# Where the weight parts of the Strassen-like products begin in their tiles: 208 bytes in place of 64

## The chip, the cores and the metric

The kernel runs on one core of one Trainium2 chip. The metric is the device time of one execution in microseconds (us), as the median of several runs. The page names five engines: PE (TensorE, matrix products), PEld (the same engine's weight loads, which overlap its products), DVE (VectorE), ACT (ScalarE) and POOL (GpSimd). SP issues most transfers.

## The reference, cut to what matters

The model is a decoder trunk with two layers over 512 tokens of width 1024. The first layer mixes tokens with a gated delta rule, the second with sliding-window attention, and both also attend to 256 memory tokens. Each layer ends in a feed-forward block, which is where the change acts:

```
def swiglu(h, w_gate_up, w_down):
    gu = h @ w_gate_up
    return (jax.nn.silu(gu[..., :D_FF]) * gu[..., D_FF:]) @ w_down
...
x = x + swiglu(rms_norm(x, ln_ffn[layer]), w_gate_up[layer], w_down[layer])
```

`h` is 512 tokens by 1024, `w_gate_up` is 1024 by 5632 and `w_down` 2816 by 1024, all in float32.

## The kernel before, in words

**A product in three parts.** The kernel multiplies in a rounded float32 type (float32r). To keep the precision, each operand is split into a high part (the rounded value, written by ACT, line 148) and a low part (what the rounding left, written by DVE, line 161), and a product is the sum of three: high by high, high weight by low activation, low weight by high activation. This is `mm3`, whose products are all line 154. In each of them a block of 128 by 128 weights is the stationary operand, loaded by PEld, and the activations stream past it.

**Wide and narrow products.** Most projections stream 512 tokens at a time, so a wide product is 128x512. In the feed-forward blocks most of the gate and up columns go through another path, `quarters`: a column of weights is cut in two halves of features and the tokens in two halves, and sums and differences of the quarters take the place of some of the products, as in Strassen's method. Those products are narrow, 128x256, and their weight parts are made by `product` inside `quarters`. Each call of `product` splits one half column of weights (128x512) and then runs four `mm3`, twelve narrow products of PE. Its activations are either halves of the tiles `h` and `l`, or the tiles `T`, which hold split sums of tokens made once by `token_sums`. The results go to the PSUM banks `g`.

**The ring.** `weight` and `quarters` share tiles of two tags, `whi` and `wlo`, with three buffers each. A tile holds 1024 numbers and `SPARE` = 64 more, 4352 bytes of each partition. `weight` uses a tile from its first byte. `quarters` takes its places from `ring`: three pairs of tiles, with two places each, the first at number `SHIFT` of the tile, the second 512 numbers behind it. A place is used again after six calls.

**Where the operands lie.** In the built program the three `whi` tiles are at bytes 20416, 24768 and 29120 of each partition and the three `wlo` tiles at 33472, 37824 and 42176. Each of these leaves 192 when divided by 256, since a tile's 4352 bytes are 17 times 256. The activations `h`, `l`, `T`, and the memory tokens `mh` and `ml`, begin at addresses that leave 192 as well, and the pieces read of them lie whole multiples of 512 bytes further. So every wide product, and every narrow one over memory tokens at the kernel's start, reads weights and activations that both leave 192. In this kernel the ring's weights leave 0 (192 + 64 = 256).

**What sets the order.** Each engine works through its own instructions in the order in which the program was written; semaphores hold an instruction back until its inputs are there and its buffer is free. In `quarters` SP and POOL issue the transfers of the weight quarters (POOL's add to what is there), ACT writes the high part, DVE the low part, and PE's twelve products follow. ACT also copies some results out of PSUM (`held`, line 148, tile `fs`), and DVE joins the rest. `quarters` is called forty times, each time for two columns, and makes seven products for them: 280 calls of `product`, 3360 narrow products. Eight gate columns take the wide path instead. In each layer the ring runs in two stretches, and each is followed by the wide down projection; the seventh product of a pair comes after the next pair's first steps, so that the last one of a stretch lies inside the down projection.

Of the kernel before, what the change touches and what calls it, by code (L numbers as in the profile page):

```python
# [27 lines left out]
FT = DFF // P  # L28
EPS = 1e-6
LINE = 64  # L30
SHIFT, SPARE = 16, 64
NEG = -1e30
BASE = 32
NB = P // BASE
# [1236 lines left out]
```

## Time and profile before

| what | value |
|---|---|
| median of 3 runs | 1158.72 us (1157.88 to 1160.98) |
| the profiled execution, its own time | 1156.72 us |
| its span | 1155.0 us |
| granted TensorE clock | 0.998 |

The span runs from the first to the last instruction; the profiled execution's own time is 1.72 us longer. The page lists busy times and shares by engine, the same in 40 slices, the chain of work that ended last, and the costliest groups. A busy time of PE is the union of products that overlap: a narrow product is shown as 0.28 us long, but one starts about every 0.12 us. What counts for PE is therefore the distance between two starts, called pitch below.

### The profile page before, as it was taken

The numbers are of one execution on the slowest core, as the hardware profiler recorded it, in microseconds if no ns is written. First come the engines' busy times: TensorE is split into PE (matmuls) and PEld (weight loads), VectorE is DVE, ScalarE is ACT, GpSimd is POOL, SyncE is SP. The second block draws the span as 40 slices with busy tenths as digits, with TensorE's granted clock in tenths as the row PEclk, the third lists the DMA queues.
The fourth block names the chain that finished last, engine by engine and source line by source line (L and its number), as shares of the span: only waits on it lengthen the run. The fifth ranks groups of instructions, "written<-read, shape, count | busy, mean of one in ns | idle before, by whom it ended". The sixth has DMA issues, their size and how long they took to land.

```text
span 1155.0 us, 19665 instructions
## 1 busy us (share of the span) xinstructions
PE 1131.5 (98%) x7476; PEld 992.9 (86%) x7476; DVE 842.6 (73%) x1587; ACT 631.7 (55%) x1271; POOL 86.0 (7%) x97
## 2 busy tenths in 40 slices
PE   7999999999999999999999999999999999999996
PEld 6888778887899998899998777777899988999986
DVE  6754877767789987389866767859799843898754
ACT  7579563366556652256654547675566522566533
POOL 0310000000101100011100000010011100111000
PEclk9999999999999999999999999999999999999999
DMA  8434342225657744567723421144477733577232
GB/s 309 133 106 117 113 103 98 92 92 165 168 139 190 188 123 126 154 147 188 178 70 104 137 73 38 51 107 126 110 188 191 183 109 105 141 183 188 72 94 94
DMA packets 73971, 152.83 MB, mean 132 GB/s; under 512 B 17756, under 2 KB 18420, under 8 KB 73876
## 3 DMA queue, kind: packets, MB, share of 16 engines
q1 hardware_dynamic: 62356, 130.59, 36.2%
q0 software_dynamic: 11520, 20.98, 11.7%
q8 instruction: 59, 0.97, 0.4%
q14 instruction: 36, 0.29, 0.1%
HBM read 144.58 MB, written 6.96 MB: 131 GB/s over the span
## 4 chain that ended last, share of the span: by engine, by line
PE 85%; DVE 8%; ACT 3%; DMA 3%; issue 1%; SPq 0%; DVEq 0%; ACTq 0%
PE pj L154 40%; PE g L154 38%; PE sc L154 5%; DVE wlo L161 2%; ACT sm L142 1%; PE pt L158 1%; DMA wraw<-in_wout 1%; PE qk L154 1%; ACT whi L148 1%; PE g L158 1%; DVE l L164 1%; DMA wraw<-in_wmk 1%; DVE btmp L161 1%; DVE stats L778 1%; DVE big L161 1%
## 5 line engine op out<-in xcount | busy, mean ns | idle before, releaser
L148 ACT ACTIVATE whi<-wraw 128x512 fp32r<-128x512 f32 (+2 forms) x331 | 244.1, 745 | 256.1 <-PE pj L154 155.9
L161 DVE TENSOR_TENSOR wlo<-wraw,whi 128x512 fp32r<-128x512 f32 (+2 forms) x331 | 274.6, 839 | 104.6 <-ACT whi L148 98.6
L154 PE MATMUL pj<-h,whi 128*128 128x512 f32 (+1 forms) x676 | 266.5, 396 | 0.0
L154 PE MATMUL pj<-l,whi 128*128 128x512 f32 (+1 forms) x676 | 264.9, 392 | 0.5 <-DVE l L164 0.4
L154 PE MATMUL pj<-h,wlo 128*128 128x512 f32 (+1 forms) x676 | 264.3, 391 | 0.0
L154 PE MATMUL g<-T,whi 128*128 128x256 f32 x1280 | 230.2, 281 | 0.0
L154 PEld LDWEIGHTS g<-T,whi 128*128 128x128 f32 x1280 | 197.5, 190 | 1.7 <-DVE fu L164 1.7
L154 PE MATMUL g<-T,wlo 128*128 128x256 f32 x640 | 179.9, 281 | 0.0
L154 PEld LDWEIGHTS pj<-h,whi 128*128 128x128 f32 x676 | 126.8, 188 | 29.2 <-issue 3.6
L154 PEld LDWEIGHTS pj<-l,whi 128*128 128x128 f32 x676 | 127.2, 188 | 27.8 <-issue 1.8
L154 PEld LDWEIGHTS pj<-h,wlo 128*128 128x128 f32 x676 | 127.1, 188 | 25.6 <-issue 0.8
L154 PE MATMUL g<-l,whi 128*128 128x256 f32 (+1 forms) x508 | 146.1, 288 | 0.0
L154 PE MATMUL g<-h,whi 128*128 128x256 f32 (+1 forms) x508 | 146.0, 287 | 0.0
L154 PE MATMUL g<-h,wlo 128*128 128x256 f32 (+1 forms) x508 | 145.9, 287 | 0.0
L154 PEld LDWEIGHTS g<-T,wlo 128*128 128x128 f32 x640 | 120.2, 188 | 0.0
L154 PEld LDWEIGHTS g<-l,whi 128*128 128x128 f32 x508 | 97.4, 192 | 1.4 <-issue 0.2
L154 PEld LDWEIGHTS g<-h,whi 128*128 128x128 f32 x508 | 95.4, 188 | 1.2
L154 PEld LDWEIGHTS g<-h,wlo 128*128 128x128 f32 x508 | 95.4, 188 | 1.0
L1014 POOL DMA_DIRECT2D ws<-in_wgu x40 | 35.4, 884 | 700.9 <-ACT sq L151 244.5
L148 ACT ACTIVATE whi<-ws 128x512 fp32r<-128x512 f32 x80 | 50.5, 631 | 51.3 <-PE g L154 42.1
L161 DVE TENSOR_TENSOR fu<-pj,rstd 128x512 f32<-128x512 f32 (+1 forms) x34 | 22.4, 660 | 54.3 <-PE pj L154 54.3
L161 DVE TENSOR_TENSOR wlo<-ws,whi 128x512 fp32r<-128x512 f32 x80 | 54.9, 686 | 6.9 <-ACT whi L148 6.8
(345 smaller groups left out, 1617.2 us busy)
## 6 DMA issues: line engine op xcount, KB each, us to landing
wraw<-in_wgu SPq DMA_DIRECT2D x48, 512.0 KB, 4.3
ws<-in_wgu SPq DMA_DIRECT2D x80, 256.0 KB, 3.7
ws<-in_wgu POOLq DMA_DIRECT2D x80, 256.0 KB, 4.8
wraw<-in_wdn SPq DMA_DIRECT2D x48, 384.0 KB, 3.1
wraw<-in_win SPq DMA_DIRECT2D x26, 512.0 KB, 3.6
wraw<-in_wgu SPq DMA_DIRECT2D x40, 256.0 KB, 4.2
wraw<-in_wout SPq DMA_DIRECT2D x16, 512.0 KB, 3.7
wraw<-in_wdn SPq DMA_DIRECT2D x16, 256.0 KB, 2.7
```

What stands on the lines that cost most here:

```text
L142: ins = self.nc.scalar.activation(out, in_, func, **kw).ins
L148: self.copied = self.nc.scalar.activation(out, in_, AF.Copy, **kw).ins
L154: return self.nc.tensor.matmul(out, lhsT, rhs, start=start, stop=stop, skip_group_check=more).ins
L158: return self.nc.tensor.transpose(out, in_, self.ident[:k, :k]).ins
L161: return eng.tensor_tensor(out=out, in0=a, in1=b, op=op).ins
L164: self.nc.vector.scalar_tensor_tensor(out=out, in0=in0, scalar=scalar, in1=in1, op0=op0, op1=op1)
L778: nc.vector.tensor_reduce(out=mx[:, i:i + 2], in_=ps[b], op=ALU.max, axis=AX.X)
L1014: nc.gpsimd.dma_start(s1, a22, accum_op=ALU.add)
```

## The change: what it does, and the diff

`SHIFT` goes from 16 to 52 numbers. The ring's places then begin at bytes 208 and 2256 of their tiles in place of 64 and 2112. The tiles keep their size (the second place ends at number 1076 of 1088), so no tile moves, and no other operand does. The ring's weights then leave 400 - 256 = 144 when divided by 256, and their activations, at 192, lie 48 bytes further on modulo 256; before it was 192. The 280 high parts that ACT writes, the 280 low parts of DVE and the 3360 narrow products that read them get other addresses. The instructions of all engines, their order and their semaphores stay as they are.

```
-SHIFT, SPARE = 16, 64
+SHIFT, SPARE = 52, 64
```

The one place that uses it (line 898, in `ring`):

```
places.extend(tuple(x[:, SHIFT + i * T:SHIFT + (i + 1) * T] for x in two) for i in range(2))
```

## The prediction

> **What bounds the kernel now.** I read the engines first, then the chain, then PE's groups by form.
>
> ```profile
> span 1155.0 us, 19665 instructions
> PE   7999999999999999999999999999999999999996
> PEclk9999999999999999999999999999999999999999
> PE 85%; DVE 8%; ACT 3%; DMA 3%; issue 1%; SPq 0%; DVEq 0%; ACTq 0%
> PE pj L154 40%; PE g L154 38%; PE sc L154 5%; DVE wlo L161 2%; ACT sm L142 1%; PE pt L158 1%; DMA wraw<-in_wout 1%; PE qk L154 1%; ACT whi L148 1%; PE g L158 1%; DVE l L164 1%; DMA wraw<-in_wmk 1%; DVE btmp L161 1%; DVE stats L778 1%; DVE big L161 1%
> ```
>
> PE is busy in nearly every slice at the full granted clock, and 85% of the chain is PE. Its two great parts are the wide products (pj, 40%) and the products into g (38%), which are nearly all the ring's. The groups by form count them:
>
> ```profile
> L154 PE MATMUL g<-T,whi 128*128 128x256 f32 x1280 | 230.2, 281 | 0.0
> L154 PE MATMUL g<-T,wlo 128*128 128x256 f32 x640 | 179.9, 281 | 0.0
> L154 PE MATMUL g<-h,wlo 128*128 128x256 f32 x480 | 135.0, 281 | 0.0
> L154 PE MATMUL g<-l,whi 128*128 128x256 f32 x480 | 134.9, 281 | 0.0
> L154 PE MATMUL g<-h,whi 128*128 128x256 f32 x480 | 134.9, 281 | 0.0
> ```
>
> These are 1280 + 640 + 3 x 480 = 3360 products, the ones whose weights move. All have no idle time of PE ahead of them. The windows show the four stretches in which the ring runs, and a short one inside the first:
>
> ```profile
> core 0: us, PE busy (x) PEld busy (x) DVE busy (x) ACT busy (x) POOL busy (x), PEclk, DMA share, GB/s
> 340.00:430.00 90.00, 90.00 (x767) 90.00 (x766) 80.51 (x146) 56.15 (x107) 12.96 (x15) 1.00 0.67 166
> 500.00:590.00 90.00, 90.00 (x766) 90.00 (x766) 80.18 (x144) 56.63 (x109) 12.94 (x15) 1.00 0.68 164
> 830.00:920.00 90.00, 90.00 (x767) 90.00 (x766) 80.39 (x144) 56.23 (x108) 16.32 (x19) 1.00 0.76 185
> 990.00:1080.00 90.00, 90.00 (x766) 90.00 (x765) 80.81 (x146) 56.80 (x110) 12.94 (x15) 1.00 0.67 165
> 345.00:365.00 20.00, 20.00 (x172) 20.00 (x172) 18.67 (x34) 12.55 (x24) 3.45 (x4) 1.00 0.80 193
> ```
>
> PE never stops there. Of the 767 products in the first row two began before the window, so the pitch (start to start) is 90.00 / 765 = **117.65 ns**. The other rows give the same. The ring's share of the time is 3360 x 117.65 ns = 395 us, and every nanosecond of pitch is worth 3.36 us. Whatever the change does to the time, it does by this pitch, or by making DVE (80.51 of 90 us) the bound.
>
> **Does the pitch depend on addresses at all?** The trace holds four other cases of the same kind of product. Times are starts in us.
>
> ```profile
> 28.21 0.28 PE L154 MATMUL sc<-mh,whi 128*128 128x256 f32 x1
> ...
> 33.49 0.28 PE L154 MATMUL sc<-mh,wlo 128*128 128x256 f32 x1
> ...
> 321.69 0.39 PE L154 MATMUL pj<-h,whi 128*128 128x512 f32 x1
> ...
> 332.57 0.28 PE L154 MATMUL g<-h,whi 128*128 128x256 f32 x1
> ...
> 430.09 0.40 PE L154 MATMUL pj<-h,whi 128*128 128x512 f32 x1
> ...
> 431.02 0.40 PE L154 MATMUL pj<-l,whi 128*128 128x512 f32 x1
> ...
> 924.15 0.39 PE L154 MATMUL g<-T,whi 128*128 128x256 f32 x2
> ...
> 925.17 0.40 PE L154 MATMUL pj<-h,wlo 128*128 128x512 f32 x1
> ```
>
> - Narrow products over memory tokens, weights and activations both at 192 modulo 256, so 0 apart: 44 steps between 28.21 and 33.49, 5.28 / 44 = **120.0 ns**.
> - Wide products, 0 apart as well: 48 steps from 321.69 to 332.57, 10.88 / 48 = 226.7 ns. They stream 256 columns more than those for 226.7 - 120.0 = 106.7 ns, which is 0.417 ns a column. So 256 columns alone are 106.7 ns, and both kinds lose 13.3 ns more per product, however long they are. The ring at 192 apart loses only 117.65 - 106.7 = 11.0.
> - Nine of the ring's own products after a stop of PE, at the very same addresses as the others: from 924.15 to 925.17 (a row x2 is two products), 1.02 / 9 = **113.3 ns**, a loss of 6.6. The same is seen after the stop at 431 us.
> - Wide products just ahead of such a stop: 0.93 / 4 = 232.5 ns from 430.09 to 431.02, 5.8 more than in their steady state.
>
> I read this so: while one product streams, the weights of the next are loaded, and the two readings get in each other's way by an amount that depends on how they meet. It is set by the distance of the addresses (13.3 against 11.0) and by the phase in which PE has fallen in (11.0 against 6.6, same addresses). Both can hold for a hundred us.
>
> The Trainium skill speaks against this. Its page "TensorE: Matmul & The Clock Gate", section "Step-by-step: what each phase is for", gives PE two independent read ports and says that loading the next weights takes no read bandwidth from the running product. By that rule the change is worth nothing, 1158.7 us. The rows disagree as far as they go: one form has 120.0, 117.65 and 113.3 ns.
>
> **The change part by part.** Nothing is added, removed or reordered on any queue, so there is no new wait. Three kinds of access move.
>
> *The 280 high parts of ACT and the 280 low parts of DVE* are written 144 bytes further. What a start off the 64-byte grid costs is bounded by these rows:
>
> ```profile
> L164 DVE SCALAR_TENSOR_TENSOR l<-x,gains,h 128x512 fp32r<-128x512 f32 x32 | 23.5, 747 | 1.5 <-ACT h L148 1.5
> L164 DVE SCALAR_TENSOR_TENSOR qv<-pj,gains,qv 128x511 f32<-128x511 f32 x12 | 9.0, 746 | 2.7 <-ACT qv L148 2.4
> L148 ACT ACTIVATE whi<-ws 128x512 fp32r<-128x512 f32 x80 | 50.5, 631 | 51.3 <-PE g L154 42.1 <-ACT fs L148 9.2
> L148 ACT ACTIVATE h<-fu 128x512 fp32r<-128x512 f32 x32 | 20.2, 633 | 18.6 <-DVE fu L161 9.8 <-DVE fu L164 8.8
> ```
>
> The convolution's DVE step starts 4 bytes off the grid (511 columns) and takes 746 ns against 747 on it. ACT takes 631 ns to the ring's address and 633 to `h`, at 192. I take nothing. The cover is PE: a ring product of twelve lasts 12 x 117.65 = 1412 ns, 63.7 of them fill 90 us, and DVE works 80.51 / 63.7 = 1264 ns in each, ACT 881. Even 100 ns more on either would be hidden.
>
> *The 3360 narrow products.* No row has weights and activations 48 bytes apart, or weights that start off a multiple of 64. Bounds: no loss at all, 106.7 ns, would be 36.8 us faster; 120.0 with the extra 5.8 of the disturbed wide products, 125.8 ns, 27.4 us slower. The middle rows are 113.3, 117.65 and 120.0. By nearness alone 48 is closest to distance 0 and its 120.0 ns. I nevertheless take **113.3**, as the likeliest single value: these very products have run at it, so a loss of 11.0 isn't needed by them, and the one distance measured apart from 0 loses less than 0 does, so that I expect of another one that it too keeps the two readings out of each other's way, more or less well. This is a choice between rows, not a derivation, and the chances below say so.
>
> The sum: about 30 products are at 113.3 already, so 3330 x (117.65 - 113.3) = 14.5 us less. At 113.3 a ring product lasts 1360 ns. DVE's 1264 still fits; in the busiest window (345 to 365 us) it is 18.67 / 20 x 1412 = 1318, so 97% full there, and I give back 0.5 us for waits of PE on a low part. 1156.7 - 14.0 = 1142.7 for a profiled execution. The median lies 2.0 above that execution, so **1144.7 us**.
>
> **The rivals.**
>
> *120.0 ns, slower.* What helps the ring now may be that its weights start at a multiple of 256, and not the distance. Then 144 is as bad as 192: 3360 x 2.35 = 7.9 us, 1166.6. For it: the one pitch of 117.65 has weights at 0, and all at 120.0 have 192; both readings of the rows fit equally. Against it: the same addresses also gave 113.3. It decides from a pitch of 118.7 ns on, as 0.3% (3.5 us, about what a measurement of this kernel tells from no change) is 1.0 ns of pitch.
>
> *125.8 ns, slower.* The disturbed phase of the wide products becomes the ring's steady one: 1186.1 us. Against it: no ring product in the trace shows it.
>
> *Unchanged, 1158.7.* Any distance other than 0 may be alike, and the phase then stays as it is. This also covers that the change doesn't do what it says: 48 is the distance to the activations, the weights themselves lie at 144. For it: four stretches with other tiles and activations have the same count of products, so the phase returns by itself each time. The rule of the Trainium skill above gives this time too.
>
> *Lower still.* The loss almost goes. Then DVE decides in its busiest stretch, at 1318 / 12 = 109.8 ns: 3360 x 7.8 = 26.2 us, 1132.5. The same page of the Trainium skill, section "Back-to-back issue gap", gives N / 2.4 + 2.5 ns for a single product's gap; by it an estimate would be 109.2 ns, 28.4 us less. No steady row here is that short for this form.
>
> **How the numbers follow.** 113.3 ns: 0.42. Lower: 0.09. Unchanged: 0.15. 120.0 ns: 0.24. 125.8: 0.10. Faster by over 0.3% is 0.42 + 0.09 = 0.51, the same 0.15, slower 0.34. The likeliest case alone would span 1140 to 1150 (pitch 112 to 115). The range leaves out the lowest and the highest case, 0.19 together: 1137 to 1168 holds 113.3, unchanged and 120.0 with their spread.
>
> **What would show it.** In the profile of the changed kernel: the count of products in a 90 us window of a stretch is 794 + 2 at 113.3, 765 + 2 if unchanged, 750 + 2 at 120.0. Wide products must stay at 226.7 and the memory tokens' at 120.0. ACT's mean for a part of the ring (631 ns) and DVE's work per ring product (1264 ns) must stay. If they grow, or if PE gets idle time ahead of g in the stretches, my account of where the time is decided is wrong. If the pitch differs among the three products of one `mm3`, the choice of phase was wrong.

## The result, and the profile after

The changed kernel takes 1156.08 us (median of 13 runs, 1153.46 to 1158.72) against 1158.79 us before (13 runs): a ratio of 0.997, with a 95% interval from 0.9959 to 0.998. It is faster by 2.7 us, a fifth of the 14.0 forecast. The time lies inside the range of 1137 to 1168; the size of the gain was wrong.

From the page of the changed kernel, its span and the shares of the chain that ended last:

```profile
span 1151.7 us, 19665 instructions
PE 89%; DVE 6%; ACT 3%; DMA 1%; issue 1%; SPq 0%; DVEq 0%; ACTq 0%
```

PE still makes the time, with 89% of the chain. The windows of the changed kernel over the stretches of the ring, with one over wide products (440 to 490 us) as the last row:

```profile
core 0: us, PE busy (x) PEld busy (x) DVE busy (x) ACT busy (x) POOL busy (x), PEclk, DMA share, GB/s
340.00:430.00 90.00, 90.00 (x773) 89.99 (x772) 81.03 (x148) 56.58 (x108) 12.76 (x15) 1.00 0.70 169
500.00:590.00 90.00, 90.00 (x774) 90.00 (x773) 79.67 (x144) 57.54 (x110) 13.00 (x15) 1.00 0.68 165
830.00:920.00 90.00, 90.00 (x774) 90.00 (x773) 80.48 (x146) 56.30 (x107) 16.46 (x19) 1.00 0.77 183
990.00:1080.00 90.00, 90.00 (x774) 90.00 (x773) 79.86 (x144) 57.52 (x110) 12.98 (x15) 1.00 0.66 165
440.00:490.00 50.00, 50.00 (x223) 41.40 (x222) 30.20 (x46) 12.25 (x16) 3.49 (x4) 1.00 0.52 142
```

Six to eight more narrow products fit in 90 us than before, and PE still never stops. The same window over wide products in the kernel before:

```profile
440.00:490.00 50.00, 50.00 (x223) 41.41 (x222) 30.12 (x46) 12.48 (x16) 3.51 (x4) 1.00 0.52 144
```

There are 223 in both: the wide products did not change. The pitch of the ring is read from the order in time of PE's instructions (start, duration, engine, line, tiles, how many in the row):

```profile
369.60 0.39 PE L154 MATMUL g<-T,whi 128*128 128x256 f32 x2
...
371.00 0.28 PE L154 MATMUL g<-h,whi 128*128 128x256 f32 x1
...
372.40 0.28 PE L154 MATMUL g<-T,whi 128*128 128x256 f32 x1
```

From 369.60 to 371.00 one product of twelve passes, from 371.00 to 372.40 another: 1.40 / 12 = **116.7 ns**. The same comes out over a whole stretch, from its first narrow product to the wide one that follows 69 calls of `product`, 828 narrow products, later:

```profile
333.20 0.28 PE L154 MATMUL g<-h,whi 128*128 128x256 f32 x1
...
429.80 0.40 PE L154 MATMUL pj<-h,whi 128*128 128x512 f32 x1
```

That is 96.60 / 828 = 116.67 ns. In the kernel before, the rows at 332.57 and 430.09 in the prediction hold the same 828 products: 97.52 / 828 = **117.78 ns**. The 117.65 of the prediction, which the expectations below repeat, is slightly low: of the 767 products in its window three had begun earlier, not two, and 90.00 / 764 = 117.8. So the pitch fell by 1.11 ns, which is worth 3360 x 1.11 = 3.7 us. The span is 3.3 us shorter (1155.0 to 1151.7), and this execution also came to its first stretch 0.6 us later than the other, ahead of all that the change moves. The page's groups show the parts that ACT and DVE write, one line for the high parts and one for the low:

```profile
L148 ACT ACTIVATE whi<-ws 128x512 fp32r<-128x512 f32 x80 | 50.4, 630 | 49.0 <-PE g L154 40.2
L161 DVE TENSOR_TENSOR wlo<-ws,whi 128x512 fp32r<-128x512 f32 x80 | 54.9, 686 | 6.4 <-ACT whi L148 6.3
```

Their 630 and 686 ns were 631 and 686. So the gain is the pitch of the narrow products. What was left to find is what sets that pitch, and why it came out at 116.7 and not at 113.3.

### The profile page after: what moved, and what is told of

The parts are those of the page before. It is cut to its first block, busy times and chain, and to the rows that moved or that the text cites. A ratio compares the mean times of both kernels' runs of the same rounds, so it can differ in the third digit from the quotient of the medians.

```text
span 1151.7 us, 19665 instructions
## 1 busy us (share of the span) xinstructions
PE 1129.2 (98%) x7476; PEld 990.3 (86%) x7476; DVE 842.4 (73%) x1587; ACT 632.1 (55%) x1271; POOL 86.1 (7%) x97
## 4 chain that ended last, share of the span: by engine, by line
PE 89%; DVE 6%; ACT 3%; DMA 1%; issue 1%; SPq 0%; DVEq 0%; ACTq 0%
PE pj L154 43%; PE g L154 38%; PE sc L154 5%; DVE wlo L161 2%; ACT sm L142 1%; PE pt L158 1%; PE qk L154 1%; ACT whi L148 1%; PE g L158 1%; DMA wraw<-in_wmk 1%; DVE stats L778 1%; DVE l L164 0%; DMA wraw<-in_win 0%; DVE x L164 0%; DVE btmp L161 0%
## 5 line engine op out<-in xcount | busy, mean ns | idle before, releaser
L154 PEld LDWEIGHTS g<-T,whi 128*128 128x128 f32 x1280 | 194.7, 188 | 1.8 <-DVE fu L164 1.8
L154 PEld LDWEIGHTS g<-T,wlo 128*128 128x128 f32 x640 | 120.1, 188 | 0.0
```

The source lines that it names most:

```text
L154: return self.nc.tensor.matmul(out, lhsT, rhs, start=start, stop=stop, skip_group_check=more).ins
```

## The experiments

In all kernels below only the places of operands in memory differ. "Place 13" is a place of the ring that begins at number 13 of its tile. Activations lie at 192 modulo 256 and a tile at 192, so a place s has a distance of -4s modulo 256. Whole multiples of 256 can be left out: in a ring with one place, products from tiles 4352 bytes (17 times 256) apart and pieces 512 bytes apart run at one pitch.

**Many places in one kernel.** The six places of the ring need not begin at the same number:

```
-SHIFT, SPARE = 52, 64
+SHIFTS, SPARE = ((0, 4), (8, 12), (20, 24)), 64
...
-                for _ in range(3):
+                for at in SHIFTS:
                     two = self.parts()
-                    places.extend(tuple(x[:, SHIFT + i * T:SHIFT + (i + 1) * T] for x in two) for i in range(2))
+                    places.extend(tuple(x[:, at[i] + i * T:at[i] + (i + 1) * T] for x in two) for i in range(2))
```

> The six places of the ring begin at six numbers of their tiles: 0, 4, 8, 12, 20, 24 (distances to the activations 0, 240, 224, 208, 176, 160 bytes modulo 256). Nothing else differs from the changed kernel. Theory D (each place's pitch follows from the distance): six pitches that come back whenever the place does, 120.0 ns at 0, the others between 113 and 120. Theory A (it follows from where the weights start modulo 256, a multiple of 256 being good): all six at 120.0 or near it, none as low as 117.65. Theory P (the phase in which PE has fallen decides, whatever the address): one pitch for all six.

> Places at 28, 32, 36, 40, 44, 48 (distances 144, 128, 112, 96, 80, 64). Theory D: six pitches between 113 and 120, and if only steps of 64 bytes count, those from 28 to 40 alike and near 117.65. Theory A: all near 120.0. Theory P: one pitch for all. If some distance gives 113.3 or less, a kernel with that one alone gains over 10 us.

> Places at 16, 52, 56, 60, 2, 64 (distances 192, 48, 32, 16, 248, 0). 16 and 52 are the two kernels' own, 2 is 8 bytes off the grid of 16, 64 has the distance of 0 and starts one place higher. Theory D: 117.65 at 16, 116.7 at 52, 120.0 at 64, as in kernels that have only the one. Theory A: 117.65 at 16, 116.7 at 52, 120.0 at 64 too, so it is the other runs that tell A from D. Theory P: the controls don't come out at their own pitches.

> Places at 1, 3, 5, 6, 7, 9 (distances 252, 244, 236, 232, 228, 220), off the 16-byte steps, as place 2 was in the run of the controls (115.6 ns there, with 119.4 and 118.2 at its neighbours 0 and 4). Theory D with single numbers (4 bytes) as steps: starts off the 16-byte grid lose less, 113 to 116 ns, with the best at 8 bytes off (6). Rival: place 2 is a single good value, and these lie at 117 to 120 as their neighbours do.

> Places at 10, 11, 13, 14, 15, 17 (distances 216, 212, 204, 200, 196, 188). Theory D with steps of 4 bytes: 10 and 14, 8 bytes off the 16-byte grid, come out as place 2 did, near 115.6 or less, the others between that and 118. Rival: all between 117 and 119, as 8, 12, 16 and 20 are.

> Places at 49, 50, 51, 53, 54, 55 (distances 60, 56, 52, 44, 40, 36), the change's neighbours at 4 bytes. Theory D with a pitch for each distance and no smooth course between: some lie 2 ns or more from the 116.7 of 52, on both sides of it. Rival (a smooth valley around 48 bytes): all between 116 and 118.

Each call of `product` is a block of twelve products at one place. The pitch of a block is taken over the nine steps from its third product on, and the table gives the median over the 44 to 48 blocks that a place has in a run (read so, the kernel before has 117.8 and the changed one 116.8):

| run | place: pitch in ns | time, us |
|---|---|---|
| e1 | 0: 119.3, 4: 118.2, 8: 118.4, 12: 117.8, 20: 118.8, 24: 118.6 | 1161.45 |
| e2 | 28: 120.1, 32: 120.0, 36: 118.2, 40: 119.6, 44: 118.0, 48: 117.8 | 1160.15 |
| e3 | 16: 117.8, 52: 117.0, 56: 116.8, 60: 117.8, 2: 115.6, 64: 120.0 | 1156.49 |
| e5 | 1: 118.7, 3: 116.2, 5: 119.7, 6: 121.3, 7: 116.6, 9: 120.0 | 1159.38 |
| e6 | 10: 118.9, 11: 117.1, 13: 113.3, 14: 117.4, 15: 118.2, 17: 118.3 | 1158.44 |
| e10 | 49: 117.8, 50: 116.7, 51: 123.0, 53: 117.3, 54: 120.0, 55: 120.8 | 1161.63 |

The kernel before stood beside these at 1157.65 us (e1 to e6) and 1158.72 (e10). Places keep their own pitches when they alternate, so theory P in its plain form (one pitch for all) falls. The controls 16, 52 and 64 come out at their own values, to 0.3 ns; but place 0, at the same distance as 64, has 119.3. There is no smooth course: 51 and 52 are 6 ns apart, 50 and 51 as much within one run, and neither the 16-byte grid nor single numbers order the values. All lie between 113.3 and 123.0. The order of the places never changes within a run, so a value may belong to a place or to the place behind its predecessor; this table can't tell which.

**Distance or start?** The right end of the memory begins with a small tile; made larger, it moves `T` (with the other tiles of that side) but not `h`:

```
-            pool("edge", side="right").tile([P, 8], F32, name="edge")
+            pool("edge", side="right").tile([P, 24], F32, name="edge")
```

> The small tile at the right end has 24 columns in place of 8, so that the tiles T, with the others of the right side, lie 64 bytes lower, at 128 modulo 256, while h stays at 192; places at 0, 16, 48, 52, 32, 64. So one place gives two distances: to h 0, 192, 64, 48, 128, 0, to T 192, 128, 0, 240, 64, 192. Theory D: place 48 has 120.0 with T and another pitch with h; places 0 and 64 have 120.0 with h and 117.65 with T. Theory A: each place has one pitch, whether it meets h or T. Theory P: one pitch for all.

Place 48 in this run, first with `T` (distance 0), then with `h` (distance 64), in order of time:

```profile
352.79 0.40 PE L154 MATMUL g<-T,whi 128*128 128x256 f32 x2
...
354.23 0.40 PE L154 MATMUL g<-T,whi 128*128 128x256 f32 x2
...
361.35 0.28 PE L154 MATMUL g<-h,whi 128*128 128x256 f32 x1
...
362.76 0.40 PE L154 MATMUL g<-T,whi 128*128 128x256 f32 x2
```

The weights are at the same addresses, and twelve products take 1.44 us with `T` and 1.41 with `h`: 120.0 and 117.5 ns. It is not `T` or `h` as such: in e2 both lay at distance 64 from place 48, and both ran at 117.8. Nor is it where ACT and DVE write, since they write place 48 at the same bytes in both cases. So theory A (the start of the weights) falls: where the two operands lie to each other counts. That their **distance** sums this up fits three of them, which kept their pitch though both operands lay elsewhere: 240 had 118.2 here (place 52 with `T`) as in e1 (place 4), 64 had 117.8 with `T` and with `h`, and 0 had 118.8 to 120.0. It doesn't fit 128, which had 118.4 and 118.8 where e2 had 120.0. And distance 192 showed that one distance can have two pitches. Place 0 with `T`, distance 192, ran at 113.3 in some blocks and at 117.8 in others:

```profile
350.36 0.39 PE L154 MATMUL g<-T,whi 128*128 128x256 f32 x2
...
351.38 0.28 PE L154 MATMUL g<-h,whi 128*128 128x256 f32 x1
```

This is the end of one such block: 1.02 / 9 = 113.3. Its predecessor had distance 0; behind a place at distance 64 the same distance of 192 had 117.8. But the predecessor's distance doesn't choose by itself: place 16 with `h`, at 192 too, ran at 117.8 also behind a place at distance 0. The run took 1160.70 us.

**One place for the whole ring, and a way in.** These differ from the changed kernel in `SHIFT` alone (2, 13), or in the first product of a stretch (its place begins at 0, all others at 16):

> The whole ring at 2 (8 bytes into the tiles, distance 248). If a place's pitch is its own, as theory D has it, 115.6 ns in all stretches: 3360 x (117.65 - 115.6) = 6.9 us less than the kernel before, 1151. If the 115.6 came from what stood beside it in the mixed run (theory P), another pitch.

> The whole ring at 13 (52 bytes into the tiles, distance 204), the place that had 113.3 ns in every block of the mixed run. Theory D: 113.3 ns in all stretches, 3360 x (117.65 - 113.3) = 14.6 us less than the kernel before, 1144, a ratio of 0.987; DVE then has 1264 ns of work in a ring product of 1360 and doesn't hold PE up. Rival (113.3 lived on the neighbours in the mixed run, or DVE becomes the bound): a pitch of 115 or more, or idle time of PE ahead of g.

> The ring at 16, as in the kernel before (distance 192), but the first of a stretch's products reads weights that begin at the tile's first byte (distance 0); the 69 behind it read them at 16. In the run with the right side moved, places at distance 192 ran at 117.8 ns behind a place at distance 64 and at 113.3 behind one at 0 or 128. Theory P' (a distance allows for several lasting phases, and the way into it chooses one): 113.3 ns through all stretches, 14 us less than before, 1144. Rival (a distance has one pitch, and 113.3 fades after a product or two): 117.65 from the second or third product on, no change of time.

Each time the window from 340 to 420 us, first of the ring at 2 (e7):

```profile
340.00:420.00 80.00, 80.00 (x695) 80.00 (x694) 73.73 (x135) 51.26 (x98) 12.97 (x15) 1.00 0.72 174
```

The ring at 13 (e9):

```profile
340.00:420.00 80.00, 80.00 (x669) 80.00 (x668) 72.55 (x130) 50.24 (x96) 12.22 (x15) 1.00 0.70 169
```

The ring at 16 behind one product at 0 (e8):

```profile
340.00:420.00 80.00, 80.00 (x682) 80.00 (x681) 72.89 (x131) 50.53 (x97) 12.94 (x15) 1.00 0.72 174
```

Such a count can be off by one product in some 700. Taken from start to start over 64 calls of `product` (768 products), the pitches are 115.6, 120.0 and 117.8 ns, the same in all four stretches. Place 2 held its pitch (1151.35 us in one run, 6.3 below one of the kernel before beside it). Place 13 did not. It ran at **120.0**, and the kernel took 1165.31 us, a ratio of 1.0064 (1.005 to 1.0078) to the kernel before: theory D as I had put it failed. And a first product at distance 0 left the ring at 117.8 (1158.81 us).

**The wide products.** The tiles of `weight` begin in turn at other numbers, with the ring at 13:

```
-            hi, lo = (x[:, :n] for x in self.parts())
+            self.turn = getattr(self, "turn", -1) + 1
+            at = WIDE[self.turn % len(WIDE)]
+            hi, lo = (x[:, at:at + n] for x in self.parts())
```

> The ring at 13, and the tiles of the wide path begin in turn at numbers 0, 2, 3, 13, 16, 48, 52 of their tiles. If the loss is a thing of how a load meets a stream, the wide products' 13.3 ns change with the place too: 226.7 at 0, and other values down to 220 (a loss of 6.6) at others, not at the same places as in the ring, since the load takes half of a wide stream only. Rival (it concerns narrow products alone, whose load and stream are equally long): 226.7 at all places.

The mean pitch of a wide tile's products (median over tiles) was 227.9 at 0, 230.7 at 2, 230.4 at 3, 233.3 at 13, 233.2 at 16, 228.9 at 48 and 232.1 ns at 52. So wide products depend on the place too, and theirs at 0 is the best of the seven. The kernel still took only 1151.27 us, since its ring, at the very addresses of e9, did this (the windows of its first two stretches):

```profile
340.00:420.00 80.00, 80.00 (x709) 80.00 (x708) 74.92 (x138) 51.80 (x99) 12.93 (x15) 1.00 0.74 177
...
500.00:580.00 80.00, 80.00 (x708) 80.00 (x708) 73.73 (x133) 52.14 (x102) 12.98 (x15) 1.00 0.75 181
```

This is 113.3 ns in place of 120.0, and so it was in all four stretches. Inside the stretches nothing was different; only what ran ahead of them was. A distance thus allows more than one lasting pitch, and the way into a stretch chooses.

**A way in chosen on purpose.** In e6 the ring went from the wide products to places 10, 11 and 13. Here the first two products of each stretch have 10 and 11, and all others one place:

```
+            n = len(turns)
+            turns.append(n)
+            t, i = places[n % 6]
+            at = WAY[n] if n < len(WAY) else SHIFT
+            return tuple(x[:, at + i * T:at + (i + 1) * T] for x in tiles[t])
```

> The ring at 13 (distance 204) but for the first two products of each stretch, which read weights at 10 and 11, as the first two did in the run with places 10 to 17, where 13 behind 11 ran at 113.3 ns every time. With the whole ring at 13 it ran at 120.0 throughout. Theory P' (a distance allows several lasting phases; the way in chooses one, and it stays for a stretch): 113.3 ns from the third product on, about 14 us less than the kernel before, 1144, ratio 0.987. Rival (the pitch belongs to the ring's mixture, every place being entered anew each time): it falls back to 120.0 within a few products, 1165 as with all at 13.

> The changed kernel's ring (52, distance 48) entered by the same two products at 10 and 11. If distance 48 allows one lasting phase only, 116.7 ns as in the changed kernel, 1155. If the prediction's 113.3 was missed only for want of the right way in, 113.3, and 1144.

> The ring of the kernel before (16, distance 192) entered by the same two products at 10 and 11. Its trace has 113.3 ns behind a stop of PE and 117.65 otherwise. Theory P': one of the two through each stretch, 113.3 (1144 us) or 117.65 (1158); the way in by a place at distance 0 left it at 117.65. Rival (113.3 at 192 lives only behind a stop): 117.65.

The same window of the ring at 13 with this way in (e12):

```profile
340.00:420.00 80.00, 80.00 (x708) 80.00 (x708) 74.98 (x137) 51.56 (x100) 12.93 (x15) 1.00 0.73 176
```

Of the changed kernel's ring at 52 (e13):

```profile
340.00:420.00 80.00, 80.00 (x688) 80.00 (x687) 73.45 (x133) 51.05 (x98) 12.93 (x15) 1.00 0.73 173
```

And of the ring at 16, as in the kernel before (e14):

```profile
340.00:420.00 80.00, 80.00 (x708) 80.00 (x708) 75.21 (x139) 52.34 (x101) 12.09 (x14) 1.00 0.69 171
```

| ring | entered from the wide products | entered by 10, 11 | time so, us |
|---|---|---|---|
| 13 (distance 204) | 120.0 ns (e9) | 113.3 | 1145.42 (e12, 4 runs) |
| 16 (192), as before | 117.8 | 113.3 | 1143.76 (e14, one run) |
| 52 (48), the change | 116.7 | 116.7 | 1154.43 (e13, one run) |

The pitches are again from start to start. e12 has a ratio of 0.9881 (0.9857 to 0.9904) to the kernel before, whose median was 1159.43 us beside these three; its 1145.42 us lie below those of both kernels. e14 is the more telling one: but for two products in each of the four stretches its weights lie where the kernel before has them, and it takes 15.7 us less than that kernel beside it. DVE is busy for 75.21 of 80 us there (94%) and doesn't hold PE up in the window.

## Why the prediction was right or wrong

- **The pitch decides, at 3.36 us for each nanosecond:** right. The pitch fell by 1.11 ns, worth 3.7 us, and the span by 3.3. The pitch before was read as 117.65 where it was 117.78, one product too many in the window, which changes no step of the argument.
- **ACT and DVE don't mind the place:** right, 630 and 686 ns; wide products stayed at 223 in 50 us.
- **The loss depends on the distance of the operands and on a phase:** right as far as the runs go. e4 showed that both operands' places count (one place, two pitches), e9 against e11 and e12 the phase (same addresses, 120.0 and 113.3). That distance alone names the first is open, as 128 in e4 doesn't fit.
- **"I nevertheless take 113.3":** this step failed. The 113.3 ns were a second phase of distance 192. The kernel before had it only behind three stops of PE, for about nine products each time (behind a fourth, at 595.63 us, it ran at 117.8), so its trace didn't show that it lasts; e14 did. I carried it over to a distance at which it was never seen. Distance 48 gave 116.7 in the changed kernel and with the way in that brings 192 and 204 to 113.3, and 116.8 to 117.0 in mixed runs. No way in that was tried brought it to 113.3. The mechanism was right, and the gain per product was put at 4.35 ns where it was 1.11.
- **The sign on the three products of one `mm3`** came out, against the choice of phase. The starts in the trace are kept to 1 ns, and in the changed kernel the steps are 117, 115, 117 and 118 ns in turn. At 113.3 (e12) they are 113 or 114 nearly throughout.
- **"By nearness alone", 120.0**, which I set aside, was no better: 48 gave 116.7. In the table 50, 51 and 52 differ by 6 ns, so a row for one distance gives no bound for its neighbour.
- **The rival on the start of the weights** fell with e4. **Unchanged** ("Any distance other than 0 may be alike") fell with the table. **125.8** was not seen, the highest being 123.0, and **Lower still** at none of the 36 places tried, the lowest being 113.3.
- The Trainium skill's rule on two independent read ports ("TensorE: Matmul & The Clock Gate", "Step-by-step: what each phase is for") does not account for this: one form of product, with nothing but places changed, had pitches from 113.3 to 123.0 ns.

What stays open: why a distance has the pitches it has, and what about a way in selects one. That weight loads and streamed reads collide is argued from the distance, which joins just these two operands; no run took the loads away.

## What to carry to other kernels

Where PE is the bound and each product loads new weights, the pitch of products is worth reading from start to start, and comparing across places of one form. If the same addresses show two pitches, the cheaper gain may be in the way into the stretch and not in the addresses. Neither can be worked out from a neighbour: a mixed run, with each buffer at another place, measures six places at once, but place 13 had 113.3 ns there and 120.0 in a ring of its own. And even a ring of one place tells its pitch only for the way in that it has.

## What the runs showed of the hardware that was not expected

- A phase lasts: with weights and activations 204 bytes apart modulo 256, narrow products ran at 120.0 ns through whole stretches (e9), or at 113.3 (e11, e12), by what ran ahead of them.
- Places 4 bytes apart differed by up to 6 ns of pitch in mixed runs (51 and 52: 123.0 and 117.0).
- A steady pitch can be the mean of unequal steps that come back in turn: 118, 122 and 120 ns at distance 204 in e9 (120.0), 117, 115, 117 and 118 at distance 48 in the changed kernel (116.7).
- Wide products lose by it as well: 226.7 ns in the steady state at distance 0, tiles up to 233.3 on the mean at others.
